# Reordering the opening of a two-layer decoder step: x transposed channel by channel, its squares summed where it lands

## The chip, the core and the metric

The kernel runs on one core of a Trainium2 chip. The metric is the device time of one execution in microseconds (us). Five engines work side by side, each through its own list of instructions in order: TensorE (PE in the profile, with its weight loads apart as PEld), VectorE (DVE), ScalarE (ACT), GpSimd (POOL) and SyncE (SP), which here only issues DMAs. ACT and POOL issue DMAs too.

## What is computed

One inference step over 512 prompt tokens and 8 sample tokens of width 1024, in a model of two layers. In each layer three sub-blocks add to x: a SwiGLU at half weight, a mixer (causal pooling in layer 0, sliding-window attention in layer 1), and a second SwiGLU. Each begins with an RMSNorm. What matters here is the very first norm and SwiGLU:

```python
def _rmsnorm(x, g):
    xf = x.astype(jnp.float32)
    y = xf * lax.rsqrt(jnp.mean(xf * xf, axis=-1, keepdims=True) + EPS)
    return (y * g.astype(jnp.float32)).astype(x.dtype)

def _swiglu(x, wg, wu, wd):
    return (jax.nn.silu(x @ wg) * (x @ wu)) @ wd

x = x + 0.5 * _swiglu(_rmsnorm(x, norm_g[l, 0]), ffn_w_gate[l, 0], ffn_w_up[l, 0], ffn_w_down[l, 0])
```

The inner width of the SwiGLU is 2816, that is 22 tiles of 128.

## The kernel before

**Layout.** x lives in SBUF transposed: eight tiles `x[k]` of 128 channels by 520 tokens (512 of the prompt, then 8 samples). In HBM tokens come first. So the opening loads the prompt in eight pieces `xt[c, b2]` (256 tokens as 2 x 128 partitions, 256 channels), the samples as `xs`, and turns them with PE into PSUM (L633, L629), from where DVE and ACT copy them to `x[k]` (L634, L636, L638). The norm weights, 72 rows of 128 numbers in `grow`, are turned the same way first (L624) into the columns `gT`.

**Precision.** Products run in a rounded fp32 type. Each operand is split into a high part, made by ACT, and the rest, made by DVE: `wh`/`wl` for weights (L187, L188), `hh`/`hl` and `xh`/`xl` for what is multiplied with them (L237 to L241). A product is three matmuls per half of the tokens, so one weight tile by one channel tile is six matmuls of 128x260.

**The first SwiGLU.** The first two gate/up tiles don't wait for the norm: they use x times the norm weight alone (`mov0`) and multiply by `R` afterwards (L466, L468). `R` holds 1/rms of each token in all 128 partitions. It is made thus: ACT squares each `x[k]` (L357), DVE adds the squares to `acc` (L359, L361), PE sums `acc` over the partitions into one column per 128 tokens (L372, `rstd_tok`), DVE takes the inverse root in some ten small steps (L376 to L383), makes diagonal matrices of it (L391, L393), and PE spreads them over the partitions (L392, L394, `rstd_all`), whence ACT copies them to `R` (L395, L396). With R, DVE makes the normalised operands for all further tiles (`normalised`, L511 to L528, with the sums and differences that the later tiles use). The third tile is a plain one on these operands; from the fourth on, a tile is made of seven products on sums of blocks (`strassen_tile`, `product`, L430), for which the weights are added up as well (L149, L150 by accumulating DMAs on POOL; L155, L159 by DVE).

**Order.** `start_hooks` is a list of steps that `plain_tile` takes one by one between its matmuls: nothing twice, `rstd_tok`, `rstd_all`, then pieces of `normalised`. The program text isn't the final order: a planner simulates the program and issues on each engine what is ready in its own timeline, by priority of the text, and each engine then keeps that order. DMAs marked `later` keep their order in the queue. PSUM is used in four double banks (`duo`), handed round.

**Weights.** `Weights` streams chunks of 1 MB through three buffers by DMAs on SP (L251), splits pieces five ahead, and the first chunk is cut into four transfers so that it can lie between the pieces of x.

Of the kernel before, what the change touches and what calls it, by code (L numbers as in the profile page):

```python
# [18 lines left out]
P = 128  # L19
# [185 lines left out]
def yoco_step(ctx, tc, ins, outs):  # L205
# [18 lines left out]
    def ps():  # L224
        return duo()[:, 0, :]
# [137 lines left out]
    pss_ = [None]  # L363
    nsb = [4]

    def rstd_tok():

        pss_[0] = duo()
        pss = pss_[0][:, 0, :]
        for t in range(5):  # L370
            lo = t * P if t < 4 else 400
            T.matmul(pss[:, t : t + 1], acc[:, lo : lo + P], ones[:, 0:1], start=True, stop=True)  # L372
        v = cp.tile([P, 5], F32, tag="nv", name="nv")
        y = cp.tile([P, 5], F32, tag="ny", name="ny")
        t1 = cp.tile([P, 5], F32, tag="nt", name="nt")
        V.tensor_scalar(v, pss[:, :5], 1.0 / D, EPS, op0=ALU.mult, op1=ALU.add)  # L376
        V.tensor_scalar(y.bitcast(I32), v.bitcast(I32), 1, None, op0=ALU.arith_shift_right)
        V.tensor_scalar(y.bitcast(I32), y.bitcast(I32), -1.0, float(0x5F3759DF), op0=ALU.mult, op1=ALU.add)
        for it in range(3):
            V.tensor_tensor(t1, y, y, op=ALU.mult)  # L380
            V.scalar_tensor_tensor(t1, t1, -0.5, v, op0=ALU.mult, op1=ALU.mult)
            o = r_tok[:, :5] if it == 2 else y
            V.scalar_tensor_tensor(o, t1, 1.5, y, op0=ALU.add, op1=ALU.mult)  # L383

    def rstd_all(pool):

        dg2 = pool.tile([P, NS], F32, tag="dg2", name="dg2", bufs=1)
        pr, pr2 = pss_[0][:, 1, :], pss_[0][:, 0, 8 : 8 + NS]
        for t in range(4):
            dg = pool.tile([P, P], F32, tag="dg", name="dg", bufs=4)  # L390
            V.tensor_scalar(dg, ident, r_tok[:, t : t + 1], None, op0=ALU.mult)  # L391
            T.matmul(pr[:, t * P : (t + 1) * P], ones, dg, start=True, stop=True)  # L392
        V.tensor_scalar(dg2, ident[:, 112:120], r_tok[:, 4:5], None, op0=ALU.mult)  # L393
        T.matmul(pr2, ones, dg2, start=True, stop=True)  # L394
        S.copy(R[:, :SP], pr)  # L395
        S.copy(R[:, SP:], pr2)  # L396
# [40 lines left out]
        split(hp, g)  # L437
        hs.append(hp)

    def plain_tile(tmp, mov, hs, scaled, hooks, steady=False):  # L440

        pg, pu = duo(), duo()
        if scaled or steady:
            for k0 in (0, 4):
                for banks in (pg, pu):
                    w = W.get()
                    W.prefetch()
                    for k in range(k0, k0 + 4):
                        mm(w, k - k0, mov[k], banks, k == 0, k == KT - 1)
                    if hooks:  # L450
                        hooks.pop(0)()
        else:

            ws = [W.get() for _ in range(4)]
            for k in range(4):
                for kk in (k, k + 4):
                    for i, banks in enumerate((pg, pu)):
                        mm(ws[2 * (kk // 4) + i], k, mov[kk], banks, kk == 0, kk == KT - 1)
                if k == 3:
                    W.prefetch()  # L460
                if hooks:
                    hooks.pop(0)()
        g = tmp.tile([P, TOK], F32, tag="g", name="g")
        t = tmp.tile([P, TOK], F32, tag="t", name="t")
        if scaled:
            V.tensor_tensor(halves(g), pg[:, :, :H], halves(R), op=ALU.mult)  # L466
            S.activation(t, g, AF.Silu)
            V.scalar_tensor_tensor(halves(g), pu[:, :, :H], -1.0, halves(R), op0=ALU.mult, op1=ALU.mult)  # L468
            V.tensor_tensor(g, g, t, op=ALU.mult)
            hidden(g, hs, tmp)  # L470
        else:
            S.activation(halves(t), pg[:, :, :H], AF.Silu)
            V.scalar_tensor_tensor(halves(g), pu[:, :, :H], -1.0, halves(t), op0=ALU.mult, op1=ALU.mult)
            hidden(g, hs)
# [56 lines left out]
    def ffn(fi, tmp, first_mov, scaled, hooks, xx, tt, after, before_last=None):  # L531
        j = 0
        for pi, n in enumerate(PARTS):
            last = pi == len(PARTS) - 1
            hs = []
            for _ in range(n):
                if j == (NU if scaled else NPL[fi]):
                    while hooks:
                        hooks.pop(0)()
                if j < NPL[fi]:  # L540
                    raw = scaled and j < NU
                    plain_tile(tmp, first_mov if raw else [xx[k] for k in range(KT)], hs, raw, hooks, j > NU)
                else:
                    strassen_tile(tmp, xx, tt, hs)
                j += 1
            nk = (n + 1) // 2
            for m0 in range(0, KT, 2):
                banks = {m: duo() for m in (m0, m0 + 1)}
                if m0 == 0:
                    late = []  # L550
                    for m in (0, 1):
                        for k0, k1 in ((0, nk), (nk, n)):
                            w = W.get()
                            for k in range(k0, min(k1, n - 1)):
                                mm(w, k - k0, hs[k], banks[m], k == 0, False)
                        late.append((w, m))
                    for w, m in late:
                        mm(w, n - 1 - nk, hs[n - 1], banks[m], False, True)
                    W.prefetch()
                for m in (m0, m0 + 1):  # L560
                    if m0:
                        mm_tile(hs, banks[m])
                    xm = halves(x[m])
                    V.scalar_tensor_tensor(xm, banks[m][:, :, :H], -0.5, xm, op0=ALU.mult, op1=ALU.add)  # L564
                    if last:
                        if before_last is not None:
                            next(before_last, None)
                        after(m)
# [12 lines left out]

        return f

    def start_hooks(tmp, n, xx, tt, late=0):

        steps = normalised(tmp, n, range(4), xx, tt)

# [1 line left out]
            for _ in range(i):  # L589
                next(steps, None)  # L590

        return [lambda: None] * (1 + late) + [rstd_tok, lambda: rstd_all(tmp)] + [lambda i=i: some(i) for i in NSTEP[late:]] + [lambda: some(100)]


    mov1 = []
    with ff_pool() as tmp:
        grow = tmp.tile([72, P], F32, tag="g", name="grow")
        nc.scalar.dma_start(grow[0:48, :], norm_g.rearrange("l n (k p) -> (l n k) p", p=P))
        xs = [big.tile([NS, 512], F32, tag=t, name="xs") for t in XX]
        for i in range(2):  # L600
            nc.scalar.dma_start(xs[i], x_sample[:, 0, i * 512 : (i + 1) * 512])
        nc.scalar.dma_start(grow[48:56, :], kv_norm_g.rearrange("(k p) -> k p", p=P))
        nc.scalar.dma_start(grow[56:64, :], final_norm_g.rearrange("(k p) -> k p", p=P))
        nc.scalar.dma_start(grow[64:72, :], pool_scale.rearrange("l (k p) -> (l k) p", p=P))
        sinks = cp.tile([P, 64], F32, name="sinks")
        nsinks = cp.tile([P, 64], F32, name="nsinks")
        sink_s = cp.tile([P, 2], F32, name="sink_s")
# [4 lines left out]
        for c in range(4):  # L612
            for b2 in range(2):
                xt[c, b2] = big.tile([P, 2, 256], F32, tag=TT[b2], name="xt")
                eng = nc.scalar if b2 and c < 2 else nc.sync
                later(eng.dma_start(xt[c, b2], xv[:, 2 * b2 : 2 * b2 + 2, c * 256 : (c + 1) * 256]))
            if c in (0, 2):
                W.begin(2)
        W.load(2)
        mov0, xx, tt = [], {}, {}  # L620
        for k in range(KT):
            if k == 0:
                pg = duo()
                T.transpose(pg[:, 0, :72], grow, ident[:72, :72])  # L624
                S.copy(gT, pg[:, 0, :72])
                px = pg[:, 1, :]
                for i in range(KT):
                    o = px[:, i * NS : (i + 1) * NS]
                    T.transpose(o, xs[i // 4][:, (i % 4) * P : (i % 4 + 1) * P], ident[:NS, :NS])  # L629
            pk = ps()  # L630
            for b in range(NB):
                src = xt[k // 2, b // 2][:, b % 2, (k % 2) * P : (k % 2 + 1) * P]
                T.transpose(pk[:, b * P : (b + 1) * P], src, ident)  # L633
            V.tensor_copy(x[k][:, SP:TOK], px[:, k * NS : (k + 1) * NS])  # L634
            if k % 2:
                V.tensor_copy(x[k][:, 0:SP], pk)  # L636
            else:
                S.copy(x[k][:, 0:SP], pk)  # L638
            z = pair(HH, [P, TOK])
            split(z, x[k], gcol(0, k))  # L640
            mov0.append(z)
        for k in range(KT):
            square(k, tmp, "g")

        prep = {}
        sel = cp.tile([P, 34], F32, name="sel")
# [43 lines left out]
                if i % 2:  # L690
                    yield

        ffn(0, tmp, mov0, True, start_hooks(tmp, 0, xx, tt, 1), xx, tt, deferred(1, tmp, "g", XX, mov1, TW), pool_prep())

    with tc.tile_pool(name="pm", bufs=2) as pm:
        for k in range(KT):
# [589 lines left out]
```

## Time and profile before

| | |
|---|---|
| median of 3 runs | 1733.42 us (1732.65 to 1733.76) |
| profiled execution | 1735.1 us, its span 1733.3 us |
| busy share of the span | PE 96%, weight loads 95%, DVE 73%, ACT 48%, POOL 8% |
| mean granted clock of PE | 0.984 |
| first matmul, on the norm weights | 8.07 us |
| first gate/up tile (L406) starts | 15.41 us |
| first use of R on DVE (L466) | 38.44 us |
| last wait of PE for a normalised operand in the opening | until 58.43 us |

The profile is of one execution, with all times from the start of its span. A group of instructions is named by line, engine, operation and tile; "idle before" is how long the engine stood ahead of them, and the arrow says whose end released it. Matmuls are pipelined, so the duration of one (0.28 us for 128x260) is longer than the spacing of two.

### The profile page before, as it was taken

How to read it: one execution, taken by the hardware profiler on the slowest of the kernel's cores; microseconds unless marked ns; L12 is line 12 of the kernel's file. 1: busy time of each engine (PE TensorE's matmuls, PEld its weight loads, DVE VectorE, ACT ScalarE, POOL GpSimd, SP SyncE). 2: the span in 40 equal slices, each digit the busy share in tenths (PEclk: the TensorE clock that was granted, in tenths of full speed). 3: DMA queues.
4: the chain of work that ended last, by engine and by line, in shares of the span. 5: the costliest groups of instructions: out<-in, count | busy, mean ns of one | idle time of the engine just before them, and what ended most of it. 6: DMA issues, size and time to landing. Idle time of an engine off the chain costs nothing.

```text
span 1733.3 us, 34536 instructions
## 1 busy us (share of the span) xinstructions
PE 1669.1 (96%) x13749; PEld 1653.5 (95%) x13749; DVE 1268.6 (73%) x2481; ACT 830.3 (48%) x1624; POOL 138.7 (8%) x170
## 2 busy tenths in 40 slices
PE   7899999999999999999999999998889999999996
PEld 7899999999899999999999999997879999999996
DVE  6974975977884874978675865878856896685784
ACT  5542543565552542554443533555866453453453
POOL 0001101100001101100101101100000110110100
PEclk9999999999999999999999999999979999999998
DMA  7455745662455755543745845542112545574631
GB/s 197 115 148 129 177 141 132 179 181 70 95 146 144 171 147 128 141 134 85 163 138 137 192 130 139 146 140 69 26 25 74 116 116 148 136 185 125 154 100 50
DMA packets 312608, 223.92 MB, mean 129 GB/s; under 512 B 9073, under 2 KB 288729, under 8 KB 312407
## 3 DMA queue, kind: packets, MB, share of 16 engines
q1 hardware_dynamic: 283760, 173.77, 35.2%
q0 software_dynamic: 22048, 39.72, 13.8%
q10 hardware_dynamic: 6638, 8.23, 1.5%
q8 instruction: 108, 1.77, 0.4%
q14 instruction: 54, 0.43, 0.1%
HBM read 179.84 MB, written 5.04 MB: 107 GB/s over the span
## 4 chain that ended last, share of the span: by engine, by line
PE 88%; DVE 7%; ACT 2%; DMA 1%; issue 1%; SPq 0%; ACTq 0%; DVEq 0%
PE ps L430 42%; PE ps L406 41%; DVE sm L983 1%; ACT sm L998 1%; DVE xl L238 1%; PE ps L1039 1%; PE ps L741 1%; PE ps L716 1%; DVE hl L238 1%; DVE tl L238 1%; DVE wl L188 0%; DMA S<-raw 0%; PE ps L372 0%; DVE xb L511 0%; PE ps L1016 0%
## 5 line engine op out<-in xcount | busy, mean ns | idle before, releaser
L187 ACT ACTIVATE wh<-raw 128x512 fp32r<-128x512 f32 (+1 forms) x734 | 441.3, 618 | 719.7 <-PE ps L406 378.5
L188 DVE TENSOR_TENSOR wl<-raw,wh 128x512 fp32r<-128x512 f32 (+1 forms) x734 | 483.4, 673 | 173.4 <-ACT wh L187 165.9
L430 PE MATMUL ps<-th,wh 128*128 128x260 f32 x1200 | 338.6, 282 | 1.9 <-ACT wh L187 1.9
L430 PE MATMUL ps<-tl,wh 128*128 128x260 f32 x1200 | 338.3, 282 | 0.0
L430 PE MATMUL ps<-th,wl 128*128 128x260 f32 x1200 | 337.3, 282 | 0.5 <-DVE wl L188 0.5
L406 PE MATMUL ps<-hh,wh 128*128 128x260 f32 x1600 | 323.0, 283 | 0.8 <-ACT R L396 0.7
L406 PE MATMUL ps<-hl,wh 128*128 128x260 f32 x1600 | 322.6, 283 | 0.0
L406 PE MATMUL ps<-hh,wl 128*128 128x260 f32 x1600 | 322.3, 283 | 0.0
L430 PE MATMUL ps<-xh,wl 128*128 128x260 f32 x900 | 254.3, 283 | 0.0
L430 PE MATMUL ps<-xh,wh 128*128 128x260 f32 x900 | 254.1, 282 | 0.0
L430 PE MATMUL ps<-xl,wh 128*128 128x260 f32 x900 | 253.7, 282 | 0.0
L406 PEld LDWEIGHTS ps<-hh,wh 128*128 128x128 f32 x1600 | 246.7, 189 | 1.1 <-ACT R L396 0.8
L406 PEld LDWEIGHTS ps<-hh,wl 128*128 128x128 f32 x1600 | 247.1, 189 | 0.0
L406 PEld LDWEIGHTS ps<-hl,wh 128*128 128x128 f32 x1600 | 247.1, 189 | 0.0
L430 PEld LDWEIGHTS ps<-th,wh 128*128 128x128 f32 x1200 | 225.6, 188 | 2.1 <-ACT wh L187 2.1
L430 PEld LDWEIGHTS ps<-th,wl 128*128 128x128 f32 x1200 | 225.5, 188 | 0.7 <-DVE wl L188 0.7
L430 PEld LDWEIGHTS ps<-tl,wh 128*128 128x128 f32 x1200 | 226.1, 188 | 0.0
L430 PEld LDWEIGHTS ps<-xh,wl 128*128 128x128 f32 x900 | 169.5, 188 | 0.0
L430 PEld LDWEIGHTS ps<-xl,wh 128*128 128x128 f32 x900 | 169.5, 188 | 0.0
L430 PEld LDWEIGHTS ps<-xh,wh 128*128 128x128 f32 x900 | 169.5, 188 | 0.0
L150 POOL DMA_DIRECT2D raw<-raw x75 | 64.9, 866 | 1169.0 <-DMA raw<-in_ffn_w_up_dram 407.1
L564 DVE SCALAR_TENSOR_TENSOR x<-ps,x 128x520 f32<-128x520 f32 x96 | 66.9, 698 | 115.7 <-PE ps L406 115.7
(230 smaller groups left out, 2345.8 us busy)
## 6 DMA issues: line engine op xcount, KB each, us to landing
raw<-in_ffn_w_gate_dram SPq DMA_DIRECT2D x87, 512.0 KB, 4.0
raw<-in_ffn_w_up_dram SPq DMA_DIRECT2D x87, 512.0 KB, 5.5
raw<-in_ffn_w_down_dram SPq DMA_DIRECT2D x32, 1024.0 KB, 5.1
raw<-raw POOLq DMA_DIRECT2D x75, 256.0 KB, 3.3
S<-in_ffn_w_up_dram SPq DMA_DIRECT2D x75, 256.0 KB, 5.6
S<-raw POOLq DMA_DIRECT2D x75, 256.0 KB, 4.3
raw<-in_ffn_w_down_dram SPq DMA_DIRECT2D x16, 768.0 KB, 4.5
raw<-in_w_q_dram SPq DMA_DIRECT2D x8, 512.0 KB, 4.7
```

Of the source, the lines that this page charges most:

```text
L150: G.dma_start(blk(raw, 2, 1), blk(raw, 1, 1), accum_op=ALU.add)
L187: nc.scalar.activation(dh, src, AF.Copy)
L188: nc.vector.tensor_tensor(dl, src, dh.bitcast(F32), op=ALU.subtract)
L238: V.tensor_tensor(lo, src, hi.bitcast(F32), op=ALU.subtract)
L406: T.matmul(banks[:, hf, :H], a[:, kk, :], hcols(b, hf), start=(first and i == 0), stop=(last and i == 2),)
L430: T.matmul(bank[:, :H], a[:, kk, :], b, start=(kk == 0 and i == 0), stop=(kk == 3 and i == 2))
L564: V.scalar_tensor_tensor(xm, banks[m][:, :, :H], -0.5, xm, op0=ALU.mult, op1=ALU.add)
L716: T.matmul(o, a[:, s], b[:, kk, :], start=(n == 0), stop=(n == 5))
L741: T.matmul(po[:, half * 256 : half * 256 + 256], z[:, tau, c], b, start=(i == 0), stop=(i == len(lst) - 1),)
L983: V.tensor_tensor_reduce(out=sm[:, e * 256 : (e + 1) * 256], in0=self.pe[e][:, bi * 256 : (bi + 1) * 256], in1=cst[:, mk : mk + 256], op0= ...
L998: S.activation(part(i), part(i), AF.Exp, bias=nm[:, i : i + 1], accum_out=den[:, i : i + 1])
L1039: T.matmul(po[:, bi * 256 : (bi + 1) * 256], a, p_[:, kc_], start=(n == 0), stop=(n == 3 * len(kts) - 1),)
```

## The change

- The five small loads of samples and later norm weights go from ACT's DMA queue to POOL's; all eight pieces of x go to SP's queue (two were on ACT's). A one-column square loads ACT's table early.
- For each k, the four prompt pieces and the sample piece are transposed into one double bank, and one copy takes all 520 columns to `x[k]`. The 48 rows of norm weights that are needed soon are transposed behind the first k; the others at the end.
- The squares are no longer taken from `x[k]`. ACT squares the loaded pieces, where tokens lie in partitions, and sums along the channels in the same instruction (16 of 128x256, 2 of 8x512) into `ss0`. One reduction over four columns then replaces the eight additions on DVE and the matmuls of L372.
- The first tile takes the channels in order: for each k, gate and up one after the other, with two weight pieces held at a time. The hooks are taken at every second k.

```diff
-    def rstd_tok():
+    def rstd_tok(ss=None):
         pss_[0] = duo()
-        pss = pss_[0][:, 0, :]
-        for t in range(5):
-            lo = t * P if t < 4 else 400
-            T.matmul(pss[:, t : t + 1], acc[:, lo : lo + P], ones[:, 0:1], start=True, stop=True)
+        if ss is None:
+            ss = pss_[0][:, 0, :]
+            for t in range(5):
+                lo = t * P if t < 4 else 400
+                T.matmul(ss[:, t : t + 1], acc[:, lo : lo + P], ones[:, 0:1], start=True, stop=True)
...
-        V.tensor_scalar(dg2, ident[:, 112:120], r_tok[:, 4:5], None, op0=ALU.mult)
+        V.tensor_scalar(dg2, ident[:, s0 : s0 + NS], r_tok[:, 4:5], None, op0=ALU.mult)
...
-        if scaled or steady:
+        if first:
+            for k0 in (0, 4):
+                ws = [W.get(), W.get()]
+                W.prefetch()
+                for k in range(k0, k0 + 4):
+                    for w, banks in zip(ws, (pg, pu)):
+                        mm(w, k - k0, mov[k], banks, k == 0, k == KT - 1)
+                    if hooks and k % 2:
+                        hooks.pop(0)()
+        elif scaled or steady:
...
         nc.scalar.dma_start(grow[0:48, :], norm_g.rearrange("l n (k p) -> (l n k) p", p=P))
+        warm = cp.tile([P, 1], F32, name="warm")
+        S.activation(warm, ones[:, 0:1], AF.Square)
...
-            nc.scalar.dma_start(xs[i], x_sample[:, 0, i * 512 : (i + 1) * 512])
-        nc.scalar.dma_start(grow[48:56, :], kv_norm_g.rearrange("(k p) -> k p", p=P))
...
+            nc.gpsimd.dma_start(xs[i], x_sample[:, 0, i * 512 : (i + 1) * 512])
+        nc.gpsimd.dma_start(grow[48:56, :], kv_norm_g.rearrange("(k p) -> k p", p=P))
...
-                eng = nc.scalar if b2 and c < 2 else nc.sync
-                later(eng.dma_start(xt[c, b2], xv[:, 2 * b2 : 2 * b2 + 2, c * 256 : (c + 1) * 256]))
+                later(nc.sync.dma_start(xt[c, b2], xv[:, 2 * b2 : 2 * b2 + 2, c * 256 : (c + 1) * 256]))
...
+        ss0 = cp.tile([P, 5, 4], F32, name="ss0")
+        V.memset(ss0, 0.0)
+        s0 = cp.tile([P, 5], F32, name="s0")
         for k in range(KT):
-            if k == 0:
-                pg = duo()
-                T.transpose(pg[:, 0, :72], grow, ident[:72, :72])
-                S.copy(gT, pg[:, 0, :72])
-                px = pg[:, 1, :]
-                for i in range(KT):
-                    o = px[:, i * NS : (i + 1) * NS]
-                    T.transpose(o, xs[i // 4][:, (i % 4) * P : (i % 4 + 1) * P], ident[:NS, :NS])
-            pk = ps()
+            pk = duo().rearrange("p a c -> p (a c)")
             for b in range(NB):
                 src = xt[k // 2, b // 2][:, b % 2, (k % 2) * P : (k % 2 + 1) * P]
                 T.transpose(pk[:, b * P : (b + 1) * P], src, ident)
-            V.tensor_copy(x[k][:, SP:TOK], px[:, k * NS : (k + 1) * NS])
+            T.transpose(pk[:, SP:TOK], xs[k // 4][:, (k % 4) * P : (k % 4 + 1) * P], ident[:NS, :NS])
+            if k == 0:
+                pg = ps()
+                T.transpose(pg[:, :48], grow[:48, :], ident[:48, :48])
+                V.tensor_copy(gT[:, :48], pg[:, :48])
             if k % 2:
-                V.tensor_copy(x[k][:, 0:SP], pk)
+                V.tensor_copy(x[k], pk[:, :TOK])
             else:
-                S.copy(x[k][:, 0:SP], pk)
+                S.copy(x[k], pk[:, :TOK])
             z = pair(HH, [P, TOK])
             split(z, x[k], gcol(0, k))
             mov0.append(z)
-        for k in range(KT):
-            square(k, tmp, "g")
+        pg = ps()
+        T.transpose(pg[:, :72], grow, ident[:72, :72])
+        V.tensor_copy(gT[:, 48:72], pg[:, 48:72])
+        for c in range(4):
+            for b in range(NB):
+                sq = tmp.tile([P, 256], F32, tag="t", name="sq")
+                S.activation(sq, xt[c, b // 2][:, b % 2, :], AF.Square, accum_out=ss0[:, b, c : c + 1])
+        for i in range(2):
+            sq = tmp.tile([NS, 512], F32, tag="t", name="sq")
+            S.activation(sq, xs[i], AF.Square, accum_out=ss0[:NS, 4, i : i + 1])
+        def norm0():
+            V.tensor_reduce(s0, ss0, axis=AX.X, op=ALU.add)
+            rstd_tok(s0)
...
-        ffn(0, tmp, mov0, True, start_hooks(tmp, 0, xx, tt, 1), xx, tt, deferred(1, tmp, "g", XX, mov1, TW), pool_prep())
+        ffn(0, tmp, mov0, True, start_hooks(tmp, 0, xx, tt, 1, [norm0, lambda: rstd_all(tmp, 0)]), xx, tt, deferred(1, tmp, "g", XX, mov1, TW), pool_prep())
```

More of the change, by code (lines that the diff above doesn't have):

```diff
@@ L375, in rstd_tok @@
         t1 = cp.tile([P, 5], F32, tag="nt", name="nt")
-        V.tensor_scalar(v, pss[:, :5], 1.0 / D, EPS, op0=ALU.mult, op1=ALU.add)
+        V.tensor_scalar(v, ss[:, :5], 1.0 / D, EPS, op0=ALU.mult, op1=ALU.add)
         V.tensor_scalar(y.bitcast(I32), v.bitcast(I32), 1, None, op0=ALU.arith_shift_right)
@@ L383, in rstd_tok, with rstd_all @@
             V.scalar_tensor_tensor(o, t1, 1.5, y, op0=ALU.add, op1=ALU.mult)
-    def rstd_all(pool):
+    def rstd_all(pool, s0=112):
         dg2 = pool.tile([P, NS], F32, tag="dg2", name="dg2", bufs=1)
@@ L438, in hidden, with plain_tile @@
         hs.append(hp)
-    def plain_tile(tmp, mov, hs, scaled, hooks, steady=False):
+    def plain_tile(tmp, mov, hs, scaled, hooks, steady=False, first=False):
         pg, pu = duo(), duo()
-        if scaled or steady:
+        if first:
[8 more added lines that the diff above has]
+        elif scaled or steady:
             for k0 in (0, 4):
@@ L541, in ffn @@
                     raw = scaled and j < NU
-                    plain_tile(tmp, first_mov if raw else [xx[k] for k in range(KT)], hs, raw, hooks, j > NU)
+                    plain_tile(tmp, first_mov if raw else [xx[k] for k in range(KT)], hs, raw, hooks, j > NU, (fi, j) == (0, 0))
                 else:
@@ L582, in deferred, with start_hooks @@
         return f
-    def start_hooks(tmp, n, xx, tt, late=0):
+    def start_hooks(tmp, n, xx, tt, late=0, norm=None):
         steps = normalised(tmp, n, range(4), xx, tt)
@@ L590, in some @@
                 next(steps, None)
-        return [lambda: None] * (1 + late) + [rstd_tok, lambda: rstd_all(tmp)] + [lambda i=i: some(i) for i in NSTEP[late:]] + [lambda: some(100)]
+        norm = norm or [rstd_tok, lambda: rstd_all(tmp)]
+        return [lambda: None] * (1 + late) + norm + [lambda i=i: some(i) for i in NSTEP[late:]] + [lambda: some(100)]
     mov1 = []
@@ L598, in yoco_step @@
         nc.scalar.dma_start(grow[0:48, :], norm_g.rearrange("l n (k p) -> (l n k) p", p=P))
+        warm = cp.tile([P, 1], F32, name="warm")
+        S.activation(warm, ones[:, 0:1], AF.Square)
         xs = [big.tile([NS, 512], F32, tag=t, name="xs") for t in XX]
         for i in range(2):
-            nc.scalar.dma_start(xs[i], x_sample[:, 0, i * 512 : (i + 1) * 512])
-        nc.scalar.dma_start(grow[48:56, :], kv_norm_g.rearrange("(k p) -> k p", p=P))
-        nc.scalar.dma_start(grow[56:64, :], final_norm_g.rearrange("(k p) -> k p", p=P))
-        nc.scalar.dma_start(grow[64:72, :], pool_scale.rearrange("l (k p) -> (l k) p", p=P))
+            nc.gpsimd.dma_start(xs[i], x_sample[:, 0, i * 512 : (i + 1) * 512])
+        nc.gpsimd.dma_start(grow[48:56, :], kv_norm_g.rearrange("(k p) -> k p", p=P))
+        nc.gpsimd.dma_start(grow[56:64, :], final_norm_g.rearrange("(k p) -> k p", p=P))
+        nc.gpsimd.dma_start(grow[64:72, :], pool_scale.rearrange("l (k p) -> (l k) p", p=P))
         sinks = cp.tile([P, 64], F32, name="sinks")
```

## The prediction

> **What bounds the kernel now.** I read the page first, then the chain of waits of the first 120 us, then the busy time by stretches of the opening, and last the groups and the timeline there. On the page, the line after the span says what the chain of work that ended last is made of:
>
> ```profile
> span 1733.3 us, 34536 instructions
> ...
> PE 88%; DVE 7%; ACT 2%; DMA 1%; issue 1%; SPq 0%; ACTq 0%; DVEq 0%
> ```
>
> PE sets the end almost everywhere, so this change, which touches only the opening, is worth what it shortens before PE becomes the bound for good. The chain of the opening, columns start, duration, what:
>
> ```profile
> 1.26 3.85 DMA raw<-in_ffn_w_gate_dram
> 5.11 0.02 issue
> 5.13 2.69 DMA grow<-in_pool_scale_dram
> ...
> 10.65 4.72 PE ps L633 x26
> 15.37 0.04 issue
> 15.41 11.10 PE ps L406 x90
> ...
> 29.02 0.70 DVE acc L361
> 29.72 0.14 issue
> 29.86 1.25 PE ps L372 x10
> 31.10 5.60 PE ps L406 x33
> ...
> 58.43 2.89 PE ps L406 x12
> ```
>
> The same stretch by engines (busy us and count for PE, weight loads, DVE, ACT, POOL; then the granted clock, DMA share, GB/s):
>
> ```profile
> 0.00:8.00 8.00, 0.00 (x0) 0.00 (x0) 0.18 (x2) 1.25 (x1) 0.69 (x6) 1.00 0.72 220
> 8.00:15.40 7.40, 7.30 (x41) 6.74 (x41) 5.60 (x17) 5.39 (x12) 0.00 (x0) 1.00 1.08 306
> 15.40:27.20 11.80, 11.79 (x96) 11.59 (x96) 11.31 (x19) 10.51 (x20) 1.03 (x1) 1.00 0.81 201
> 27.20:29.80 2.60, 0.00 (x1) 0.00 (x0) 2.51 (x4) 1.01 (x2) 0.00 (x0) 1.00 0.76 206
> 31.00:34.70 3.70, 3.70 (x19) 3.70 (x20) 3.08 (x17) 0.00 (x0) 0.54 (x1) 0.54 0.77 211
> 38.40:45.00 6.60, 6.60 (x58) 6.60 (x57) 6.56 (x12) 5.00 (x9) 0.00 (x0) 1.00 0.16 44
> 45.00:58.40 13.40, 8.21 (x62) 7.39 (x61) 13.40 (x26) 6.44 (x11) 1.75 (x2) 1.00 0.53 118
> 58.40:62.00 3.60, 3.57 (x17) 3.57 (x18) 3.60 (x8) 1.81 (x3) 0.00 (x0) 0.53 0.00 0
> ```
>
> PE waits for the last norm weights, transposes x (L633), runs the first gate/up tile (L406, 96 matmuls to 27.2), stands 2.6 us for the last addition of squares, makes the token sums (L372), and goes on with the second tile. From 38.4 to 58.4 DVE is busy 19.96 of 20.0 us: it makes the normalised operands, and in 45 to 58.4 PE is busy only 8.21 of 13.4 us for want of them. So the date of 58.43, from which PE runs on, hangs on when R, the broadcast of 1/rms, reaches DVE. That date is on the DVE timeline:
>
> ```profile
> 31.14 0.16 DVE L376 TENSOR_SCALAR nv<-ps 128x5 f32<-128x5 f32 x1 [1.43 <-PE ps L372]
> ...
> 34.41 0.32 DVE L393 TENSOR_SCALAR dg<-ident,r_tok 128x8 f32<-128x8 f32 x1
> ...
> 38.44 0.70 DVE L466 TENSOR_TENSOR g<-ps,R 128x520 f32<-128x520 f32 x1 [1.67 <-ACT R L396]
> ```
>
> R is there at 38.44, and 58.43 - 38.44 = 20.0 us of DVE work follow. I forecast the shift of R and carry it to the end.
>
> **The squares.** Removed on DVE: eight additions of 0.70 us behind the squares. The last square, and the rest of ACT's work of the opening (the groups to 38.4 us, then two operations from elsewhere that price the new one, then their chain piece):
>
> ```profile
> 27.59 0.62 ACT L357 ACTIVATE sq<-x 128x520 f32<-128x520 f32 x1
> ```
>
> ```profile
> L187 ACT ACTIVATE wh<-raw 128x512 fp32r<-128x512 f32 x11 | 6.6, 628 | 8.2 <-PE ps L406 8.2
> L240 ACT ACTIVATE hh<-x,gT 128x520 fp32r<-128x520 f32 x8 | 5.5, 732 | 0.0
> L357 ACT ACTIVATE sq<-x 128x520 f32<-128x520 f32 x8 | 5.1, 637 | 0.3 <-DVE acc L361 0.3
> L638 ACT COPY x<-ps 128x512 f32<-128x512 f32 x4 | 2.3, 581 | 1.6 <-PE ps L633 1.6
> ```
>
> ```profile
> L998 ACT ACTIVATE sm<-sm,nm 128x256 f32<-128x256 f32 x64 | 31.7, 498 | 13.7 <-DVE nm L994 13.6
> L487 ACT COPY sa<-ps 128x260 f32<-128x260 f32 x75 | 26.9, 358 | 3.7 <-PE ps L430 3.7
> ```
>
> ```profile
> 1240.49 2.08 ACT sm L998 x8
> ```
>
> Now the last square ends at 27.59 + 0.62 = 28.21, and the last addition at 29.72, 1.5 us later. After the change sixteen 128x256 squares with a sum and two 8x512 ones stand on ACT instead of eight of 0.637. The trace has no such square. From above it is L998, four operations with their four reads of the sum in 2.08 us, 0.52 each; from below L487, 0.36. I take the middle, 0.44, since L998 carries a bias and L487 no sum: 16 x 0.44 + 2 x 0.63 (the price of a 512 to 520 wide one) = 8.3 us, between 7.0 and 9.6, against 5.1. [...]
>
> ACT then has, up to the last square, 2.3 (copies) + 5.5 (hh) + 9 x 0.6 = 5.4 (the weight copies that stood ahead of it, of the eleven) + 8.3 = 21.5 us. It can begin when the first half of x is in, about 5.4 (an estimate: in the chain a weight transfer issued at 1.26 ends at 5.11, and the first pieces of x are issued around it), where it now stood still to 8 but for a table load; the planner took each square as soon as it was ready, so I let ACT run without a gap: last square at 5.4 + 21.5 = 26.9, 1.3 earlier. Bounds: 25.6 to 28.2 by the price alone. The last piece of x is not the limit: 2.1 MB of x and 1.05 MB of weights stand ahead of it in both kernels, and 220 GB/s x 8 us + 306 GB/s x 4.5 us brings them by 12.5; from then on 4 squares, two hh and a copy remain.
>
> **From the squares to R.** Removed: ten matmuls (29.86, 1.25 us) and their hand-over, 31.14 - 29.72 = 1.4 us. Added: one reduction of 128x20 on DVE; nearest row is L376 at 0.16, I take 0.3 with its wait, between 0.2 and 0.5. The chain nv to dg stays (31.14 to 34.73). Then PE has the broadcast behind 33 matmuls of the second tile in its order: 31.10 + 5.60 = 36.70, though dg was ready at 34.73. These 33 took 0.170 us each against 0.123 (11.10 / 90) in the first tile, because the clock was granted at 0.54 from 31.0 to 34.7, right after the stop. 33 x 0.047 = 1.55 us. Without stop and token matmuls this goes, and I count 1.7 of the 2.0 us of that queue as gained. Bounds 0 and 2.0: where the planner puts the broadcast isn't in the trace.
>
> Sum for R: 1.3 (squares end earlier) + 1.5 (additions) + 1.4 (token matmuls) + 1.7 (queue and clock) - 0.3 (reduction) = 5.6 us, R at 32.8.
>
> **After R.** DVE's 20 us stay as they are, so 58.43 becomes 52.8. PE must have got there too: its busy time from 15.41 to 58.43 is 43.0 - 2.6 - 5.2 = 35.2 us, less 1.25 and 1.55, 32.4 us. If the first tile starts at 15 as now, PE would be ready at 47.4: DVE stays the later one by 5.4 us, about the gap of now, so I leave the cold stretch of 58.4 to 62 (0.53) as it is.
>
> **The rest, at nothing.** Transposes start at about 6 instead of 8.07, but the last x comes at 12.5 and ten transposes of 0.18 (4.72 / 26) follow; the first tile can end at 26 to 27 as now. Its order by channels has the same 96 matmuls and gives PE 12 x 0.123 = 1.5 us of work for each hh instead of 0.74, which covers late ones. Second transpose of the norm weights and gT copy: under 0.6 us on PE and DVE, where the queue after R has 5.4 us of slack on PE; without it 0.6. Five loads on POOL:
>
> ```profile
> L150 POOL DMA_DIRECT2D raw<-raw x75 | 64.9, 866 | 1169.0 <-DMA raw<-in_ffn_w_up_dram 407.1
> ```
>
> 5 x 0.87 = 4.3 us on POOL from about 1.3, and no other work there is due before POOL's own x1 in 15.4 to 27.2; if the samples landed late, PE would stand at the first channel, at worst to about the present 8 us. Two x loads go from ACT's to SP's queue: the two issues (under 1 us) fall ahead of weights that are used from 15.4 on. The table load moves to where ACT has nothing. Wider single copies save eight DVE copies of 8 columns in a stretch where ACT is the later engine.
>
> **Forecast.** The profiled execution took 1735.1 us, with its span 1733.3; the median of the three runs, 1733.4, is 1.7 below. 1735.1 - 5.6 = 1729.5, and against the median 1727.8 us. A measurement here can tell about 0.2%, 3.5 us. The likeliest case spans 3.6 to 7.6 us of gain (queue term and square price at their ends, but not all at once).
>
> **Rivals.**
> *Gain eaten by ACT's order (0.23).* The planner puts hh and weight copies ahead of the squares, with ACT standing for x in between: the last square stays at 28.2 and the queue on PE gives nothing. Then 5.6 - 1.3 - 1.7 = 2.6 us remain: 1730.8. For it: ACT is at 10.51 of 11.8 us in the first tile and gets 3.2 us more. Against: in 8 to 15.4 it worked only 5.39 of 7.4 us, and in the first 8 only 1.25.
>
> *ACT as the new bound, with a cold first tile (0.15), slower.* Squares ahead of hh: each channel then costs ACT 21.5 / 8 = 2.7 us, and PE has 1.5 us for it, 55% busy. In 45 to 58.4 PE was busy 61% and the clock fell to 0.53 right behind. At a clock of 0.54 a matmul takes 0.123 / 0.54 = 0.23 and a channel 2.7 us, so the first tile would need 22 us from about 12 on and end at 34. The broadcast, 33 matmuls and 2 us later, would give R at 34 + 4.1 + 2 = 40.1, or with the 33 cold as well (7.6 us) at 43.6: 1735.1 to 1738.6, and I take 1738.0, since a tile fed so leaves the next one cold. It decides from a first tile that ends after 32.3. [...]
>
> *More than forecast (0.12).* Squares run wholly ahead in ACT's idle start and end at 24: another 2.9 us, 1724.9. PE's readiness at 47.4 still allows it.
>
> **How the numbers follow.** Forecast 0.50, the others 0.23, 0.15 and 0.12. Faster by over 0.2%: 0.50 + 0.12 = 0.62. Within: 0.23, and 0.03 from the slower rival's lower end, 0.26. Slower: 0.12. The range goes from 1724.0 (rival of more gain) to 1735.0, which leaves out the slower rival, 0.15, and little below.
>
> **What would show it.** Right: no matmuls of L372 in the opening and no PE stop after the first tile; clock 1.00 in 27 to 35; ACT unbroken from 6 to 27; first multiplication by R at about 33; PE's last wait for xl at about 53, and the rest shifted as a whole. Wrong: R later than 35 with the squares done by 27 (PE's order), or squares ending after 28 (ACT), or a first tile at half clock, or a stretch after 70 us whose length differs from now.

## The result, and the profile after

The kernel after takes 1742.55 us (median of 5 runs, 1740.38 to 1746.73) against 1733.42 beside it: ratio 1.0054, 95% interval 1.0041 to 1.0067. Its profiled execution took 1743.55 us. I had forecast 1727.8 us with a range to 1735.0, so the sign was wrong and the miss is 14.8 us. It falls into two halves: the opening, forecast 5.6 us shorter, became 1 to 2 us longer in the profiled run, and the attention, which starts some 1100 us behind the edited part, became 7 us longer. First the page of after, its span and, below it, the shares of its last chain:

```profile
span 1741.8 us, 34550 instructions
...
PE 89%; DVE 7%; ACT 2%; issue 1%; DMA 1%; SPq 0%; ACTq 0%; DVEq 0%; POOL 0%; POOLq 0%
```

PE bounds as before. Its chain of waits in the opening (start, duration, what):

```profile
14.89 2.69 PE ps L407 x12
18.81 9.56 PE ps L407 x78
28.39 0.64 ACT wh L187
29.12 0.54 issue
29.83 0.59 DVE wl L188
32.64 0.77 PE ps L393 x2
33.40 3.47 PE ps L407 x16
36.87 1.28 PE ps L393 x6
...
59.83 2.97 PE ps L407 x12
```

The token matmuls and the additions are gone from it, as forecast. In their place stand a weight split (`wh`, `wl`), 3.57 us without matmuls, and sixteen matmuls of the second tile between one broadcast matmul (L393) and the other ones. The DVE timeline shows what the split does there:

```profile
26.04 0.17 DVE L377 TENSOR_SCALAR nv<-s 128x5 f32<-128x5 f32 x1
26.25 0.17 DVE L378 TENSOR_SCALAR ny<-nv 128x5 int32<-128x5 int32 x1
29.05 0.69 DVE L188 TENSOR_TENSOR wl<-raw,wh 128x512 fp32r<-128x512 f32 x1 [2.63 <-ACT wh L187]
29.66 0.17 DVE L379 TENSOR_SCALAR ny<-ny 128x5 int32<-128x5 int32 x1
29.74 0.68 DVE L188 TENSOR_TENSOR wl<-raw,wh 128x512 fp32r<-128x512 f32 x1
...
32.99 0.22 DVE L394 TENSOR_SCALAR dg<-ident,r_tok 128x8 f32<-128x8 f32 x1
39.10 0.70 DVE L477 TENSOR_TENSOR g<-ps,R 128x520 f32<-128x520 f32 x1 [5.89 <-ACT R L397]
```

DVE runs its list in order. Between the second and third step of the inverse root stands a `wl`, whose `wh` waits for one of the last matmuls of the first tile (ACT idles 2.59 us on PE ahead of 28.39). The root is cut in two, and PE, which has its first broadcast matmul right behind the first tile, stands. R comes at 39.10 (38.44 before). The stop and what follows it, by stretches (busy us and count for PE, weight loads, DVE, ACT, POOL; then clock, DMA share, GB/s):

```profile
29.05:32.64 3.59, 0.02 (x2) 0.04 (x1) 3.21 (x15) 0.49 (x1) 0.00 (x0) 0.91 1.05 258
32.64:38.40 5.76, 5.76 (x27) 5.76 (x28) 0.58 (x4) 0.00 (x0) 1.74 (x2) 0.50 0.54 95
45.00:59.80 14.80, 10.92 (x87) 10.31 (x85) 14.80 (x28) 7.78 (x14) 1.73 (x2) 0.98 0.54 124
```

The second row is at half clock, ahead of the broadcast; the last shows DVE full again until PE's last wait at 59.83, 20.7 us behind R.

The second half is in the attention. PE's waits in the timeline, in before and then in after, at the first softmax (the figure in brackets is the idle time):

```profile
1193.44 0.33 PE L1016 MATMUL ps<-ident,sm 128*128 128x128 f32 x1 [1.65 <-DVE sm L1006]
1196.12 0.47 PE L1016 MATMUL ps<-ident,sm 128*128 128x128 f32 x1 [2.35 <-ACT sm L1004]
```

```profile
1197.17 0.69 PE L1041 MATMUL ps<-ident,sm 128*128 128x128 f32 x2 [5.14 <-DVE sm L1031]
```

One stop of 5.14 us has taken the place of two with work between. DVE's list there, before and then after:

```profile
1192.63 0.15 DVE L1000 TENSOR_TENSOR den<-den,es 128x4 f32<-128x4 f32 x1
1192.82 0.18 DVE L1001 RECIPROCAL den<-den 128x4 f32<-128x4 f32 x1
1193.04 0.62 DVE L1006 TENSOR_SCALAR sm<-sm,den 128x256 f32<-128x256 f32 x2
```

```profile
1193.21 0.73 DVE L848 STREAM_SHUFFLE rp<-rp 128x520 f32<-128x520 f32 x1
1193.84 0.41 DVE L1008 CUSTOM_DVE_ANT_0 sm<-ps,cst 128x256 f32<-128x256 f32 x1
...
1195.21 0.15 DVE L1025 TENSOR_TENSOR den<-den,es 128x4 f32<-128x4 f32 x1
...
1195.96 0.17 DVE L1026 RECIPROCAL den<-den 128x4 f32<-128x4 f32 x1
...
1196.77 0.61 DVE L1031 TENSOR_SCALAR sm<-sm,den 128x256 f32<-128x256 f32 x2
```

The program text there is the same. Only its order on the engines differs: a shuffle and four masked maxima (L1008) of the next unit now stand ahead of `den`. From the load of the mask constants to the last `oT` copy, before takes 1163.71 to 1327.91 = 164.2 us, after 1163.95 to 1335.34 = 171.4. The instruction lists that PE, ACT and DVE ran in the two profiles, counted back from their ends, are the same except in three places: the opening (to about 115 us), this attention, and the start of the last SwiGLU. So two theories stood: the planner's new order costs the 7 us, or the opening does, by where its transfers fall later.

### The profile page after: what moved, and what is told of

It reads as the page before. It is cut to its first block, busy times and chain, and to the rows that moved or that the text cites. A ratio compares the mean times of both kernels' runs of the same rounds, so it can differ in the third digit from the quotient of the medians.

```text
span 1741.8 us, 34550 instructions
## 1 busy us (share of the span) xinstructions
PE 1680.8 (96%) x13740; PEld 1661.2 (95%) x13740; DVE 1263.4 (73%) x2469; ACT 833.1 (48%) x1652; POOL 141.0 (8%) x175
## 4 chain that ended last, share of the span: by engine, by line
PE 89%; DVE 7%; ACT 2%; issue 1%; DMA 1%; SPq 0%; ACTq 0%; DVEq 0%; POOL 0%; POOLq 0%
PE ps L431 42%; PE ps L407 41%; PE ps L1064 1%; DVE sm L1008 1%; DVE xl L238 1%; PE ps L766 1%; DVE wl L188 1%; PE ps L741 1%; DVE hl L238 1%; ACT sm L1023 1%; DVE tl L238 1%; PE ps L1041 0%; DMA S<-raw 0%; ACT wh L187 0%; DVE xb L522 0%
```

## The experiments

Each time below is a median; each ratio is to before as run beside it, whose median lay between 1732.9 and 1733.7 us. To test the first theory, each engine was given its order from outside. `pin` adds edges between successive instructions of one engine, with no semaphore, so that the planner must keep the list:

```python
def pin(nc, tc, text):
    traced = list(nc.cur_bb.bb.instructions)
    edge = lambda: mybir.DependencyInfo(mybir.DependencyClass.NoSync, mybir.DependencyReason.DATA)
    for steps in json.loads(zlib.decompress(base64.b85decode(text))):
        at = prev = None
        for d in steps:
            at = d if at is None else at + d
            if prev is not None:
                tc.add_manual_dep(traced[at], prev.name, edge(), reason="pin")
            prev = traced[at]
```

**e1: after, in the order of before behind the opening.**

```diff
         yoco_step(tc, args, outs)
+        pin(nc, tc, PLAN)
```

The lists of e1, as its profile shows them, differ from after's only in the attention and at the start of the last SwiGLU; up to there, the opening with it, they are after's own.

> The kernel after, in which each of PE, ACT and DVE keeps, from the second feed-forward tile on, the order of instructions that the kernel before has. Theory 1 (the loss is the planner's new order in the attention, where after spends 167.6 us and before 160.4): 7.2 of the 9.1 us come back, 1735.3 us, the attention lasts 160.4 +- 1, and what stays are the 2 to 3 us that the trace of after is behind by 161 us. Theory 2 (the loss comes from the opening or from where its transfers fall against later ones, and the order in the attention is only a sign of it): 1742.5, and the attention lasts 165 or more.

1735.23 us (12 runs), ratio to before 1.0003 (0.9993 to 1.0013). The attention takes 165.3 us (between the marks used above; the text put on record counted it between others, with the same difference of 7.2), and the stop at the first softmax has shrunk to 1.13 us:

```profile
1196.02 0.33 PE L1041 MATMUL ps<-ident,sm 128*128 128x128 f32 x1 [1.13 <-ACT sm L1029]
```

Theory 1: 7.3 us of the loss by the medians, 8.8 by the ratios, are the order. That the median lies within 0.1 us of the forecast is luck, as the interval is 3.5 us wide.

**e2: before, in the order of after behind the opening.** The same edit on before, with after's list.

> The kernel before, in which PE, ACT and DVE keep behind the first feed-forward tiles the order that the kernel after has. Theory 1 (the new order in the attention costs the time): 1733.4 + 7.2 = 1740.6 us, or 1741.6 with the last feed-forward part's microsecond, attention 167 to 168. Theory 2 (the order isn't the cause): 1733.4, attention 160 to 161.

1742.75 us, ratio 1.0044 (1.0030 to 1.0059), attention 171.2 us, and the same stop:

```profile
1194.31 0.69 PE L1016 MATMUL ps<-ident,sm 128*128 128x128 f32 x2 [5.13 <-DVE sm L1006]
```

Theory 1 again, with 1 to 2 us more than it said. Not one line of before's arithmetic was changed. Together with e1 this shows that the order alone makes the second half of the miss. Both runs change the order in the attention and at the start of the last SwiGLU at once. With DVE's instructions lined up against before's profile, e2 loses 7.0 us in the attention and a further 1.7 between 1345 and 1460 us, after 7.2 and 1.2, so most of it is the attention.

**e3: e1 with the two weight subtractions behind the last dg.** DVE's pinned list:

```diff
   s, nv, ny (L378)
-  wl
   ny (L379)
-  wl
   nt ... r_tok, dg, dg, dg, dg, dg2
+  wl
+  wl
```

> The first kernel of this call, and two weight subtractions (wl) on DVE, which stand among the steps of the reciprocal square root, placed behind the last dg. Theory A (DVE's wait of 2.6 us for the first of them, and its own 0.4 twice, hold R): dg is written about 3.1 us earlier, PE's stop of 3.57 us at the first broadcast matmul shrinks to about 0.5, its clock isn't halved, so that the 16 matmuls of the second tile between the broadcasts take 1.8 instead of 3.47; R reaches DVE at about 39.1 - 3.1 - 1.7 = 34.3 instead of 39.1, and the time is 4.8 below the first kernel of this call, about 1730.5. Theory B (the opening's end isn't set by R but by DVE's other work and the raw transfers): R early, time within 1 us of the first kernel of this call.

1728.39 us (8 runs, 1725.39 to 1739.13), ratio 0.9972 (0.9953 to 0.9990), 6.8 below e1 by the medians and 5.4 by the ratios: theory A, whose 4.8 lies within the noise. PE's stop and DVE's timeline, and PE's last wait:

```profile
27.17 0.46 PE L393 MATMUL ps<-dg,ones 128*128 128x128 f32 x2 [0.29 <-DVE dg L392]
```

```profile
26.45 0.17 DVE L384 SCALAR_TENSOR_TENSOR r_tok<-nt,ny 128x5 f32<-128x5 f32 x1
...
27.65 1.28 DVE L188 TENSOR_TENSOR wl<-raw,wh 128x512 fp32r<-128x512 f32 x2
31.06 0.70 DVE L477 TENSOR_TENSOR g<-ps,R 128x520 f32<-128x520 f32 x1 [2.12 <-ACT R L397]
```

```profile
51.66 0.80 PE L407 MATMUL ps<-xl,wh 128*128 128x260 f32 x2 [1.92 <-DVE xl L238]
```

R is there at 31.06, 7.2 us sooner than in e1 (38.25), and PE's last wait ends at 51.66, 20.6 behind it. This profiled run had the first tile at full pace, which e1's and after's had not (below), and its sum was ready 2.2 us sooner, ahead of the edited steps (nv at 24.23, in e1 at 26.42). That part of the 7.2 is luck of the run; the medians carry the verdict.

**e4: e3 with the five broadcast matmuls together.**

```diff
   PE: last matmul of the first tile
   L393
-  16 matmuls of the second tile
   L393, L393, L393, L395
+  16 matmuls of the second tile
```

> The kernel before this one in the call, and the broadcast's five matmuls together, right behind the first tile, rather than one of them there and four behind 16 matmuls of the second tile. Theory A (R sets the opening's end): R no longer waits for the 16 matmuls (1.8 us at full clock), so R at about 32.5 and the time 1.5 to 2 below the run before this one, about 1729; PE stands about 1 us longer ahead of the broadcasts, which is work that the second tile makes up. Theory B: no difference over 0.5 us.

1728.27 us, ratio 0.9972 (0.9959 to 0.9986): the same as e3, so theory B by the medians, though with intervals 5 to 6 us wide a gain of 1.5 us could hide in them. The profiles show why none need be expected. From nv to R it took 5.0 us instead of 6.8, as theory A said; but behind R DVE now stood 0.67 us for `wh` and 0.92 for another result of ACT, and PE's last wait ended at 52.71, 22.4 behind R instead of 20.6.

**e5, e6, e7: each part of the change alone**, on before, with before's order behind the opening (e7's planner kept that order by itself).

```diff
 e5   for k in range(KT): square(k, tmp, "g")   ->   ACT squares of xt and xs with their sums, norm0
 e6   loads, transposes and copies of after; squares, additions and L372 of before
 e7   plain_tile(..., first) only
```

> The kernel before, in which only the squares of the first norm are taken on ACT from x as it is loaded (with the reduction, without the token matmuls and the additions); transposes and first tile as before; PE, ACT and DVE keep the order of before from behind the opening on. Theory 1 (the early sum itself brings DVE's two weight subtractions into the middle of the reciprocal square root, and PE's stop at the first broadcast): a stop of 3 us or more at that matmul, R at DVE at 37.5 to 39.5 (38.44 before), and 1733 to 1735 us. Theory 2 (it takes the new transposes or the first tile's channel order to do that): no stop over 1 us, R at about 33, 1728 to 1730.

> The kernel before, in which only the loads and transposes change (x first, the samples with them, the norm weights behind); squares, additions, token matmuls and first tile as before; the order behind the opening as before. Theory 1 (the start of the transposes 4 us sooner is lost in waits for x, as PE's wait of 4.2 for xt and the cold first tile of after show): R within 0.7 of 38.44, 1733 to 1734.5 us. Theory 2 (half or more of the 4 us reaches R): R at 36.5 or earlier, 1731.5 or less.

> The kernel before, in which only the first tile's matmuls go by channels, gate and up in turn. Nothing pins it: the planner keeps by itself the order of before behind the opening. Theory 1 (with all the rest as before, the tile only changes the order in which the same matmuls run): 1733.5 +- 0.7, R within 0.5 of 38.44. Theory 2 (the channel order makes PE wait for each channel's split, and run cold): first tile 1 to 2 us longer, 1734.5 to 1736.

| | us | ratio to before (95%) | PE's stop at the broadcast | R on DVE |
|---|---|---|---|---|
| e5 squares | 1731.54 | 0.9988 (0.9979 to 0.9996) | 3.99 | 36.58 |
| e6 loads | 1730.59 | 0.9986 (0.9977 to 0.9996) | none, and none ahead of L372 | 35.45 |
| e7 first tile | 1732.74 | 0.9994 (0.9985 to 1.0002) | none (2.65 ahead of L372, as before) | 38.68 |

DVE's list of e5 has the subtractions in the root again:

```profile
27.71 0.17 DVE L378 TENSOR_SCALAR ny<-nv 128x5 int32<-128x5 int32 x1
27.82 0.69 DVE L188 TENSOR_TENSOR wl<-raw,wh 128x512 fp32r<-128x512 f32 x1
...
28.51 0.68 DVE L188 TENSOR_TENSOR wl<-raw,wh 128x512 fp32r<-128x512 f32 x1
```

So the early sum alone brings them there, as theory 1 said. But the first doesn't wait for its `wh` here, and they cost 1.2 us. The stop of 3.99 us is mostly the root itself, since nv came only at 27.51, with the end of the first tile. R is earlier than theory 1 allowed and the time below both its ends. e6 went by theory 2: the start of the transposes 4 us sooner does reach R. e7 is no change that a measurement tells. So with the rest of the order held, no part is slow, and two parts gain a little (0.12% and 0.14%); together (e1) they gain nothing that can be told.

**e8 and e9: which engine's order?** After, with PE alone in before's order behind the opening (e8), and with ACT and DVE alone (e9).

> The kernel after; behind the opening PE alone keeps the order that before has, ACT and DVE keep the order of after. Theory 1 (PE's own order costs the time: it has the first softmax's transposes ahead of other matmuls and stands at them for 5.1 us): that stop falls to about 4 in two pieces, 1736 to 1737.5 us. Theory 2 (the softmax itself is written late, because ACT and DVE put other work ahead of its exponentials and its scaling): PE stands as long or longer, 1741 to 1744.

> The kernel after; behind the opening ACT and DVE keep the order that before has, PE alone keeps the order of after (the other half of e8). Theory 1 (ACT and DVE alone decide: they write the first scaled softmax late): PE's stop of 5.1 us at the softmax's transposes falls under 3, the attention takes 165 to 167 instead of 171.4, 1735 to 1737 us. Theory 2 (either order alone holds the attention back, since each engine waits for the other's): the stop stays over 4, 1740 to 1743.

e8: 1740.45 us, ratio 1.0048 (1.0033 to 1.0063), with the stop unchanged:

```profile
1198.63 0.69 PE L1041 MATMUL ps<-ident,sm 128*128 128x128 f32 x2 [5.14 <-DVE sm L1031]
```

e9: 1742.69 us, ratio 1.0069 (1.0046 to 1.0092). Its single stop is gone, but other waits have come; three of PE's waits in the attention (total, times, longest):

```profile
PE ps L1041 <- DVE hl L238: 2.9, 3, 2.3
PE ps L1041 <- ACT sm L1029: 2.4, 1, 2.4
PE ps L1109 <- ACT oT L1076: 1.6, 1, 1.6
```

Each half of the new order is as slow as the whole, so the times of both runs went by theory 2 (e8's is 0.5 us below its range). The stop of 5.14 us goes with ACT's and DVE's lists: it stays in e8 and is gone in e9, as theory 1 of e9 said. But lists from two different orders make PE wait elsewhere, so neither run says what a single engine's list costs; the lists belong together.

**e10 and e11: e5 and e6 with nothing pinned.**

```diff
-        pin(nc, tc, PLAN)
```

> The kernel e5 with nothing pinned: the planner orders everything itself, and its order differs from that of before in the attention as after's does at the first softmax. Theory 1 (any of the three parts that shifts the planner's clock can tip the attention into the slow order): PE's stop of about 5 us at the first softmax is there, and the time is e5's 1731.5 + 7 = 1738.5 us. Theory 2 (the slow order belongs to the whole change, and this part alone gets one as good as before's): 1731 to 1733.

> The kernel e6 with nothing pinned; the planner's order differs from that of before in the attention, and in some other places. Theory 1: the stop of about 5 us at the first softmax, 1730.6 + 7 = 1737.6 us. Theory 2: an order as good as before's, 1730 to 1732.5.

1738.43 us (ratio 1.0036, 1.0022 to 1.0050) and 1738.14 us (1.0036, 1.0024 to 1.0048), 6.9 and 7.6 above the same kernels pinned (8.3 and 8.7 by the ratios). PE's wait in the attention, e10 and then e11:

```profile
PE ps L1031 <- DVE sm L1021: 5.1, 1, 5.1
```

```profile
PE ps L1017 <- DVE sm L1007: 5.1, 1, 5.1
```

Theory 1 of both. Two quite different edits of the opening, each a gain when the order is held, tip the planner into an order with the same stop in the attention, and lose 7 to 9 us by it.

**e12: e1 with the broadcast together, and the weight subtractions left in the root.** PE's edit of e4, without DVE's.

> The kernel e1, with the broadcast's five matmuls together behind the first tile, and DVE's two weight subtractions left in the middle of the reciprocal square root (the half of e4 that e3 lacks). Theory 1 (both the weight subtractions and the placing of the broadcast hold R): R at DVE at 35 to 35.5 instead of 38.25, the time 2 to 3 below e1's 1735.2, about 1732.5. Theory 2 (only the wait for the weights counts, and PE's queue is made up by the second tile): within 0.7 of e1.

1735.67 us, ratio 1.0016 (1.0000 to 1.0032): no gain over e1 (1.0003, 0.9993 to 1.0013), theory 2, though its profiled run has R at 33.35. The 2 to 3 us of theory 1 are ruled out; a gain under 1 us is not. So an early R is not enough by itself: behind it DVE waits for ACT here (0.65 and 0.92 us) as in e4, and PE's last wait ends at 55.69, 22.3 later. Of the two, the weights in the root hold the opening back: e12 keeps PE's stop of 3.57 us, e3 has 0.29.

## Why the prediction was wrong, point by point

**The squares: right, and better.** The group of squares in the opening, and the read of the sum behind the last one:

```profile
L661 ACT ACTIVATE sq<-xt 128x256 f32<-128x256 f32 x16 | 6.5, 411 | 1.5 <-DMA xt<-in_x_prompt_dram 1.5
```

```profile
25.62 0.18 ACT L664 ACTIVATION_READ_ACCUMULATOR sq<-xs 8x1 f32 x1
```

I took 0.44 each between 0.36 and 0.52; they came at a pace of 0.41, with the read of the sum (0.19) lying beside the next square. Alone the square took 0.411, under the 0.498 of L998 in before. The last sum was there at 25.80 instead of 26.9.

**Squares to the root: right.** Additions and token matmuls went, the reduction cost 0.24 us with its wait (25.80 to 26.04) where I had 0.3. By the terms of my sum nv stood at 31.14 - 1.3 - 1.5 - 1.4 + 0.3 = 27.2; it came at 26.04, 1.2 sooner.

**"The chain nv to dg stays": the first step that failed.** It was 3.6 us (31.14 to 34.73) and became 7.2 (26.04 to 33.21), by two weight subtractions of 0.6 and the 2.63 us for which DVE stood ahead of the first. I had priced the root as a block. It is twelve entries in DVE's list, and once the sum was early, the planner had weight splits to put between them; the trace of before shows splits right ahead of the root, which should have been a rival. That they were ready in the planner's own timeline is the likely reason, but only argued.

**The queue term: the second.** I counted 1.7 of 2.0 us as gained between dg and R. It was 34.73 to 38.44, 3.7 us; it became 33.21 to 39.10, 5.9: a loss of 2.2 us, outside my bounds of 0 to 2.0. A stop stood at the end of the first tile, as in before, only longer (3.57 for 2.65), and half clock (0.50) behind it, ahead of the broadcast. So R: 32.8 - 1.2 (sum earlier) + 3.6 (root) + 3.9 (queue, 2.2 lost and 1.7 not gained) = 39.1.

**"The first tile can end at 26 to 27 as now": the third.** It ended at 29.07 in after's profiled run and at 26.77 in e9's, which has the same order there. Its own first matmuls decide, at half pace in the one and not in the other (0.64 us a pair against 0.40). The split in the root waits for that tile, so its lateness goes on to R.

**"20 us of DVE work behind R": right** in after (20.7) and e3 (20.6), but not a law: 22.4 in e4, and in e6 R came 3.0 us sooner than in before and PE's last wait ended at 59.98, 1.5 later, while the operations behind it were 3 us ahead. That wait marks the end of the opening only while the lists around it stay the same.

**"The rest shifted as a whole": the step that cost most**, 7.3 us by the medians of after and e1, 7 to 9 by all the pairs (e1, e2, e10, e11). The planner made a new order in the attention, with one stop of 5.14 us, and at the start of the last SwiGLU. I had named "a stretch after 70 us whose length differs from now" as a sign of a wrong forecast, and had no rival for it, though the description of the kernel above says that a planner orders everything in its own timeline. Why its timeline tips there is not shown. Of the miss of 14.8 us, 7.3 are this one, and 6.8 come back in e3.

**The rivals.** The slower one had the sign right, 4.5 us too low, and its mechanism wrong: no first tile ended after 32.3, and the squares did not run ahead of what PE needed. That it points the right way is luck. Of the signs of being wrong, "R later than 35 with the squares done by 27" came true, but I had put it down to PE's order, and it was DVE's list. The forecast of the opening was borne out where its conditions hold: with the order held and the root unbroken (e3) the kernel takes 1728.4 us, where I had 1727.8. The interval of e3 is 6 us wide, so the closeness is luck; but in the profiles e3 and e4 stand 5.5 and 4.2 us ahead of before at 455 us, where I had 5.6.

## What to carry to other kernels

Where a planner sets the order, as here, an edit is worth what its own stretch gains plus a draw over later stretches; compare the engines' lists of both kernels before costing anything, and hold the old order when only the edit is to be measured. A chain of tiny operations has no length of its own: it is as long as what the list puts between them, above all anything that waits for another engine (nv to dg took 3.6 us in before and 7.2 in after, 2.63 of them a wait for ACT). And a first gain can be undone twice over without one slow instruction: here all parts were sound, and the version that keeps the old order and the root in one piece (e3, e4) is 0.28% faster than before and about 0.8% faster than after.

## What the hardware showed that I had not expected

**The same stop halves the clock in one run and not in another.** Of seven profiled runs with a stop of 3.57 to 3.99 us at the first broadcast, the matmuls behind it ran at half pace (0.64 us a pair, against 0.40) for the whole way to the broadcast's end in after and e9, for a part of it in e1, e5 and e10, and not at all in e8 and e12. In after and then e8, both in the same list:

```profile
35.37 0.64 PE L407 MATMUL ps<-hh,wl 128*128 128x260 f32 x2
```

```profile
32.55 0.40 PE L407 MATMUL ps<-hh,wl 128*128 128x260 f32 x2
```

The granted clock was 0.50 from 32.64 to 38.40 in after and 1.00 from 31.8 to 38.4 in e8, and R came at 39.10 in the one and at 35.64 in the other. The stop of 0.29 us in e3 didn't do it (clock 1.00 from 26.8 to 31.0), and e4 has none over 0.2. Five of the seven stops brought half pace, and after and e8 have the same stop of 3.57, so chance has a hand in it. In e10 the pace fell only some 1.2 us after the matmuls had begun again at 31.60, behind a stop of 3.96:

```profile
32.38 0.40 PE L407 MATMUL ps<-hh,wl 128*128 128x260 f32 x2
...
33.41 0.64 PE L407 MATMUL ps<-hh,wl 128*128 128x260 f32 x2
```

And behind before's shorter stop of 2.65 us, with 1.25 us of thin matmuls after it, the clock was 0.54 from 31.0 to 34.7. Behind the thin matmuls without a stop, 1.17 us of them in e6 and in e11, pairs took 0.40. What decides whether the clock falls isn't shown.

**The first tile starts at half pace by chance too.** The twelve matmuls at 14.89 took 2.69 us in after, 0.64 a pair; in e3, in the same order, pairs took 0.40 there:

```profile
16.51 0.64 PE L407 MATMUL ps<-hl,wh 128*128 128x260 f32 x2
```

```profile
14.62 0.40 PE L407 MATMUL ps<-hh,wl 128*128 128x260 f32 x2
```

The pace is the 0.64 a pair that after has at a clock of 0.50 behind its stop, but the clock column of the stretches says 1.00 for after in 14 to 18; that the clock makes it is therefore not shown, and the spacing of the matmuls has to be read beside that column. By these draws four runs with the same opening (after, e1, e8, e9) stood at +2.4, +1.4, -1.2 and +1.1 us against before at 455 us (DVE's instructions of the traces lined up): one profile of an opening is good to some 2 us.

**A transfer stall comes and goes.** Before's profiled run stood twice for weight sums near 1090 us; the chains of before and after:

```profile
1088.10 6.80 DMA S<-in_ffn_w_up_dram
1094.91 2.33 issue
1097.23 7.78 DMA S<-raw
```

```profile
1079.89 46.60 PE ps L431 x390
```

After's had none of it, and is 2.8 us to the good between 1063 and 1167; e4's had 8.95 us for `S<-raw` and lost a further 2.4, while e3, in the same order there, gained 2.8. It goes with the run and not with the order, and the 5.2 us between e3 and e4 are about as large as the gain that I was looking for.
